# Norm intermediates and the squared ReLU move from SBUF to PSUM, and scale and shift become three instructions

## The chip, the core and the metric

The kernel runs on one core of one Trainium2 chip. The metric is the device time of one execution in microseconds (us); the time of a kernel is the median of its runs. The engines are named as the profile names them: PE (TensorE, matmuls), PEld (its weight loads), DVE (VectorE), ACT (ScalarE), POOL (GpSimd) and SP (SyncE, which issues the DMAs). A matmul writes PSUM; DVE and ACT read and write both PSUM and SBUF; POOL works here on SBUF tiles alone.

## The reference, cut to what matters

128 context tokens and 512 latent tokens, each a vector of 1024 channels, go through two layers in fp32. Layer 0 mixes tokens with a gated linear recurrence in eight heads, layer 1 with a convolution module; an MLP with 4096 hidden units follows each. Ahead of each sub-layer stands a norm with a scale and a shift that differ between context and latent tokens, and a residual with a gate closes it:

```python
def rmsnorm(x, w):
    y = xf * lax.rsqrt(jnp.mean(xf * xf, axis=-1, keepdims=True) + EPS)
    return (y * w.astype(F32)).astype(x.dtype)

hp = rmsnorm(xp, norm_mlp[i]) * (1.0 + m_ctx[4]) + m_ctx[3]     # context
hs = rmsnorm(xs, norm_mlp[i]) * (1.0 + m_lat[4]) + m_lat[3]     # latent
xs = xs + m_lat[5] * sqrelu_mlp(hs, mlp_w1[i], mlp_w2[i])

def sqrelu_mlp(h, w1, w2):
    return jnp.square(jax.nn.relu(h @ w1)) @ w2

# inside the convolution module, over the channels of each token
mu = jnp.mean(uf, axis=-1, keepdims=True)
var = jnp.mean(jnp.square(uf - mu), axis=-1, keepdims=True)
uf = (uf - mu) * lax.rsqrt(var + EPS) * ln_g.astype(F32) + ln_b.astype(F32)
return jax.nn.silu(uf).astype(h.dtype) @ w_pw2
```

## The kernel before

Activations lie channel by token: 8 tiles of 128 channels (index k), 640 token columns, context first. The columns are worked in two halves, A and B: 320 and 320 up to the first norm of layer 1, and 304 and 336 behind it. Half A holds all 128 context columns, so an instruction with a scale or a shift per token kind comes there in two pieces (128 and 192, or 128 and 176 columns); in half B it is one piece (`segs`).

A linear layer runs in units of 128 output channels (`half_unit`, `unit_k`): for each of 8 k, three matmuls, since weights and activations are split in a high and a low part (wh·hi + wl·hi + wh·lo; lines 180, 183, 184). A unit is 24 matmuls into one PSUM tile `ps_mm`, of which pool `mmp` has three in turn: the fourth unit's first matmul has to wait until the first unit's tile has been read for the last time. Two more PSUM pools exist: `scp` (three tiles, tag "sc", used by the recurrence and for the taps of the convolution, `ps_cv`) and `axp` (two tiles). Weights come by DMA into `rw`; ACT rounds them to `wh` (line 161), and POOL, in some stages DVE, subtracts (`wl`, line 165).

Work beside the matmuls that no unit asks for at once stands in a list `bg` of small steps (norms, the taps of the convolution, the modulation vectors of line 128), from which `between` issues some behind each unit. A planner in the framework then orders each engine's queue ahead of time by what it takes each instruction to cost; the queues run in that order.

A norm (`rms_stat`, `inv_rms`, `norm_steps`) squares each of 8 tiles on ACT into `nsq` in SBUF (line 256), adds them up on DVE in `nacc` (257), sums over channels with a matmul by ones into `ps_n` (230), takes the root on ACT into the SBUF tile `rs` (232) and the reciprocal on DVE there (233). With `by_token` the root and reciprocal are taken on a few columns, and the result is spread by matmuls into PSUM (238 to 242). Then, per k (`apply`): DVE multiplies x by `rs` into `nt` in SBUF (278), `modulate` scales and shifts in place, on DVE for half of the k (270) and on ACT for the others (268), and `split` has ACT round to the high part (169) and DVE subtract for the low part (170; tiles ah, al for half A, bh, bl for half B).

The hidden layer's evacuation (`hid_evac`): ACT takes the ReLU of `ps_mm` into the SBUF tile `hr` (703), DVE multiplies `ps_mm` by it into `hr` (704), and `split` works on `hr` (ch, cl for half A, dh, dl for half B). The residual (287) is one DVE instruction per token kind. The layer norm of the convolution (`ln_steps`) takes the channel mean with a matmul into `ps_mu` (817), copies it scaled to SBUF `mu` on ACT (819), subtracts it in eight DVE instructions (822), takes the statistics as above, and per k multiplies by `rs` (828), applies SiLU on ACT (829) and splits, all in SBUF.

Of the kernel before, what the change touches and what calls it, by code (L numbers as in the profile page):

```python
# [45 lines left out]
CUT = 304  # L46
CA = 5
TM0 = True
ND = (1, 3, 5, 7)
ND0 = (0, 2, 4, 6)  # L50
CB = 6
COLS = (((0, HALF), (HALF, NT)), ((0, CUT), (CUT, NT)))

# [16 lines left out]
def hybrid_step(ctx: ExitStack, tc: tile.TileContext, xt, vec, pos, masks, ident_in, state, c_rows, w_mod0, w_modt,  # L70
# [16 lines left out]
    mask = const.tile([P, NMASK, SB], U8, name="mask")  # L87
    ones = const.tile([P, P], F32, name="ones")
    pool.memset(ones[:], 1.0)
    eps = const.tile([P, 2], F32, name="eps")  # L90
    pool.memset(eps[:, 0:1], EPS)
    pool.memset(eps[:, 1:2], EPS * P)
# [75 lines left out]
    def split(src, hi, lo, eng=dve):  # L168
        act.copy(hi, src)  # L169
        eng.tensor_tensor(lo, src, hi.bitcast(F32), ALU.subtract)  # L170
# [55 lines left out]
    def inv_rms(tp, acc, n, by_token):  # L226

        ps = axp.tile([P, 512], F32, tag="ax", name="ps_n")
        if not by_token:
            pe.matmul(ps[:, :n], ones[:], acc, start=True, stop=True)  # L230
            rs = tp.tile([P, HW], F32, tag="rs", name="rs")
            act.activation(rs[:, :n], ps[:, :n], AF.Sqrt, bias=eps[:, 0:1], scale=1.0 / D)
            dve.reciprocal(rs[:, :n], rs[:, :n])
            return rs[:, :n]
        c = n // 4
        rc = tp.tile([P, 4], F32, tag="rc", name="rc", bufs=2)
        for i in range(4):
            pe.matmul(ps[:c, 508 + i:509 + i], acc[:, i * c:(i + 1) * c], ones[:, 0:1], start=True, stop=True)
        act.activation(rc[:c], ps[:c, 508:512], AF.Sqrt, bias=eps[:c, 0:1], scale=1.0 / D)
        dve.reciprocal(rc[:c], rc[:c])  # L240
        for i in range(4):
            pe.matmul(ps[:, i * c:(i + 1) * c], rc[:c, i:i + 1].broadcast_to([c, P]), ident[:c, :c],
                      start=True, stop=True)
        return ps[:, :n]

    def rms_stat(tp, xs, n, by_token=False):

        box = {}

        def sq(k):  # L250
            if k == 0:
                box["acc"] = tp.tile([P, HW], F32, tag="nacc", name="nacc", bufs=2)
                act.activation(box["acc"][:, :n], xs(0), AF.Square)
            else:
                t = tp.tile([P, HW], F32, tag="nsq", name="nsq", bufs=2)
                act.activation(t[:, :n], xs(k), AF.Square)
                dve.tensor_tensor(box["acc"][:, :n], box["acc"][:, :n], t[:, :n], ALU.add)  # L257

        def fin():
            box["rs"] = inv_rms(tp, box["acc"][:, :n], n, by_token)  # L260

        return box, [(0.45, lambda k=k: sq(k)) for k in range(KT)] + [(0.3 if by_token else 2.1, fin)]

    def modulate(t, layer, which, k, lo, hi, eng=act):
        for s, a, b in segs(lo, hi):
            r, sc, bi = t[:, a - lo:b - lo], amod[:, layer, which, k, s:s + 1], mvec(layer, 3 * which, k, s)
            if eng is act:
                act.activation(r, r, AF.Identity, bias=bi, scale=sc)  # L268
            else:
                eng.tensor_scalar(r, r, sc, bi, ALU.mult, ALU.add)  # L270

    def norm_steps(tp, x, layer, which, acts, lo, hi, by_token, on_dve):
        n = hi - lo
        box, steps = rms_stat(tp, lambda k: x[:, k, lo:hi], n, by_token)

        def apply(k):
            t = tp.tile([P, HW], F32, tag="nt", name="nt", bufs=2)
            dve.tensor_tensor(t[:, :n], x[:, k, lo:hi], box["rs"], ALU.mult)  # L278
            modulate(t, layer, which, k, lo, hi, dve if k in on_dve else act)
            split(t[:, :n], acts[k][0][:, :n], acts[k][1][:, :n])  # L280

        return steps + [(0.85, lambda k=k: apply(k)) for k in range(KT)]

    def residual(x, layer, chunk):
        def evac(u, half, lo, hi, ps):
            for s, a, b in segs(lo, hi):
                dve.scalar_tensor_tensor(x[:, u, a:b], ps[:, a - lo:b - lo], mvec(layer, chunk, u, s),  # L287
                                         x[:, u, a:b], ALU.mult, ALU.add)
        return evac
# [17 lines left out]
    with tc.tile_pool(name="start", bufs=1) as st:  # L307
# [78 lines left out]
        def first_norm(k0, k1):  # L386
            for k in range(k0, k1):
                pin(dve.tensor_tensor(x0[:, k], x0[:, k], rs[:], ALU.mult), int(k > 4))
                modulate(x0[:, k], 0, 0, k, 0, NT, dve)
                for half, (lo, hi) in enumerate(COLS[0]):  # L390
                    split(x0[:, k, lo:hi], h[half][k][0][:, :HALF], h[half][k][1][:, :HALF], (dve, pool)[half])

# [306 lines left out]
    def hid_evac(hid):  # L699
        def evac(u, half, lo, hi, ps):  # L700
            n = hi - lo
            r = rp.tile([P, HW], F32, tag="hr", name="hr")
            act.activation(r[:, :n], ps, AF.Relu)
            dve.tensor_tensor(r[:, :n], ps, r[:, :n], ALU.mult)  # L704
            split(r[:, :n], hid[half][u][0][:, :n], hid[half][u][1][:, :n])
        return evac

    hid = {}
# [7 lines left out]
    def mlp_out(layer, cols, group=8, done=None):  # L716
        linear(8, hid, residual(xr, layer, 5), cols, group, done=done)

    def start_norm(layer, which, half, cols, first=True, by_token=False, on_dve=ND):

        h[half] = new_act("ab"[half])
        steps = norm_steps(tp, xr, layer, which, h[half], *cols, by_token, on_dve)
        bg[:] = steps + bg if first else bg + steps
        return steps[-1]

# [4 lines left out]

    budget[1] = 3.0
    for cols in (A0, B0):
        linear(8, on, residual(xr, 0, 2), cols, done=lambda half: start_norm(0, 1, half, COLS[0][half], False, TM0, ND0))
    drain()
    with tc.tile_pool(name="wm1", bufs=1) as wmp:
        scratch = wmp.tile([P, D], F32, name="scratch")
# [73 lines left out]
    def ln_steps(half):  # L810
        n = COLS[1][half][1] - COLS[1][half][0]
        h[half] = new_act("ab"[half])
        acts = h[half]

        def mean():
            ps = axp.tile([P, 512], F32, tag="ax", name="ps_mu")
            pe.matmul(ps[:, :n], ones[:], lnb["sum"][:, :n], start=True, stop=True)
            lnb["mu"] = cv.tile([P, HW], F32, tag="mu", name="mu")
            act.activation(lnb["mu"][:, :n], ps[:, :n], AF.Copy, scale=1.0 / D)

        def sub(k):
            dve.tensor_tensor(lnb["y"][:, k, :n], lnb["y"][:, k, :n], lnb["mu"][:, :n], ALU.subtract)  # L822

        box, steps = rms_stat(tp, lambda k: lnb["y"][:, k, :n], n)

        def fin(k):
            y = lnb["y"][:, k, :n]
            dve.tensor_tensor(y, y, box["rs"], ALU.mult)
            act.activation(y, y, AF.Silu, bias=v("ln_b")[:, k:k + 1], scale=v("ln_g")[:, k:k + 1])
            split(y, acts[k][0][:, :n], acts[k][1][:, :n])  # L830

        return ([(0.5, mean)] + [(0.4, lambda k=k: sub(k)) for k in range(KT)] + steps
                + [(0.8, lambda k=k: fin(k)) for k in range(KT)])
# [135 lines left out]
```

## Time and profile before

| | before |
|---|---|
| time, median of 3 runs (lowest to highest) | 1619.97 us (1619.37 to 1620.06) |
| the profiled execution | 1616.84 us |
| its span, first to last instruction | 1614.9 us |
| mean granted clock of TensorE | 0.989 |
| PE busy | 1578.3 us (98%) |
| DVE busy | 1249.4 us (77%) |
| ACT busy | 761.9 us (47%) |
| POOL busy | 694.0 us (43%) |
| DMA | 240.11 MB, mean 149 GB/s |

PE is busy nearly all the time, so the parts of the span that are not its own are read from what PE waited for, stretch by stretch, and from what the engine that it waited for had in its queue there. Times of day in the text ("at 811 us") count from the start of the span.

### The profile page before, as it was taken

How to read it: one execution, taken by the hardware profiler on the slowest of the kernel's cores; microseconds unless marked ns; L12 is line 12 of the kernel's file. 1: busy time of each engine (PE TensorE's matmuls, PEld its weight loads, DVE VectorE, ACT ScalarE, POOL GpSimd, SP SyncE). 2: the span in 40 equal slices, each digit the busy share in tenths (PEclk: the TensorE clock that was granted, in tenths of full speed). 3: DMA queues.
4: the chain of work that ended last, by engine and by line, in shares of the span. 5: the costliest groups of instructions: out<-in, count | busy, mean ns of one | idle time of the engine just before them, and what ended most of it. 6: DMA issues, size and time to landing. Idle time of an engine off the chain costs nothing.

```text
span 1614.9 us, 32111 instructions
## 1 busy us (share of the span) xinstructions
PE 1578.3 (98%) x12810; PEld 1536.0 (95%) x12810; DVE 1249.4 (77%) x2222; ACT 761.9 (47%) x1227; POOL 694.0 (43%) x863
## 2 busy tenths in 40 slices
PE   8999999999999999999999999999999899999997
PEld 6899999988899999999999999989999899999997
DVE  5788888878738998788789997899999686555544
ACT  3566666665446313344454334764344554334321
POOL 3100000000484765555978888789898710000000
PEclk7999999999999999999999999999999999999998
DMA  9333333333253556766544444345454344444401
GB/s 360 129 112 113 112 112 113 112 109 103 101 190 122 181 183 224 235 225 208 169 144 144 156 146 145 129 134 169 157 164 148 122 153 158 144 144 144 144 27 66
DMA packets 71302, 240.11 MB, mean 149 GB/s; under 512 B 7792, under 2 KB 14576, under 8 KB 70128
## 3 DMA queue, kind: packets, MB, share of 16 engines
q1 hardware_dynamic: 71152, 238.06, 44.4%
q8 instruction: 101, 1.65, 0.4%
q14 instruction: 49, 0.40, 0.1%
HBM read 234.36 MB, written 3.67 MB: 147 GB/s over the span
## 4 chain that ended last, share of the span: by engine, by line
PE 76%; DVE 17%; POOL 2%; ACT 2%; issue 2%; DMA 0%; SPq 0%; DVEq 0%; POOLq 0%; ACTq 0%
PE ps_mm L180 23%; PE ps_mm L184 22%; PE ps_mm L183 22%; DVE ps_cv L794 3%; POOL wl L165 2%; DVE scratch L128 2%; PE ps_sc L504 2%; DVE nt L278 1%; DVE nacc L257 1%; DVE cl L170 1%; PE ps_u L588 1%; DVE hr L704 1%; DVE nt L270 1%; DVE yc L822 1%; DVE al L170 1%
## 5 line engine op out<-in xcount | busy, mean ns | idle before, releaser
L165 POOL TENSOR_TENSOR wl<-rw,wh 128x256 fp32r<-128x256 f32 x808 | 668.8, 861 | 568.1 <-ACT wh L161 561.6
L161 ACT CAST wh<-rw 128x1024 fp32r<-128x1024 f32 x334 | 348.4, 1046 | 314.4 <-PE ps_mm L184 230.8
L180 PE MATMUL ps_mm<-bh,wh 128*128 128x320 f32 (+1 forms) x1000 | 317.8, 318 | 2.8 <-ACT nt L268 2.6
L180 PE MATMUL ps_mm<-ah,wh 128*128 128x320 f32 (+1 forms) x1000 | 311.6, 312 | 1.9 <-ACT ah L169 1.1
L183 PE MATMUL ps_mm<-bh,wl 128*128 128x320 f32 (+1 forms) x1000 | 311.4, 312 | 0.0
L184 PE MATMUL ps_mm<-bl,wh 128*128 128x320 f32 (+1 forms) x1000 | 310.8, 311 | 0.0
L184 PE MATMUL ps_mm<-al,wh 128*128 128x320 f32 (+1 forms) x1000 | 308.0, 308 | 1.7 <-DVE al L170 1.7
L183 PE MATMUL ps_mm<-ah,wl 128*128 128x320 f32 (+1 forms) x1000 | 308.0, 308 | 0.0
L794 DVE SCALAR_TENSOR_TENSOR ps_cv<-ub,vt,ps_cv 128x319 f32<-128x319 f32 (+1 forms) x464 | 228.7, 555 | 0.4
L165 DVE TENSOR_TENSOR wl<-rw,wh 128x1024 fp32r<-128x1024 f32 x132 | 168.7, 1280 | 39.6 <-ACT wh L161 39.6
L180 PEld LDWEIGHTS ps_mm<-ah,wh 128*128 128x128 f32 x1000 | 188.6, 189 | 7.3 <-issue 3.4
L180 PEld LDWEIGHTS ps_mm<-bh,wh 128*128 128x128 f32 x1000 | 188.0, 188 | 5.7 <-ACT nt L268 2.8
L183 PEld LDWEIGHTS ps_mm<-ah,wl 128*128 128x128 f32 x1000 | 188.5, 188 | 3.2 <-issue 2.6
L184 PEld LDWEIGHTS ps_mm<-al,wh 128*128 128x128 f32 x1000 | 188.6, 189 | 3.1 <-DVE al L170 2.2
L183 PEld LDWEIGHTS ps_mm<-bh,wl 128*128 128x128 f32 x1000 | 187.9, 188 | 0.5
L184 PEld LDWEIGHTS ps_mm<-bl,wh 128*128 128x128 f32 x1000 | 188.1, 188 | 0.1
L287 DVE SCALAR_TENSOR_TENSOR xr<-ps_mm,mod,xr 128x128 f32<-128x128 f32 (+2 forms) x240 | 97.8, 434 | 112.3 <-PE ps_mm L184 111.9
L180 PE MATMUL ps_mm<-ch,wh 128*128 128x320 f32 (+1 forms) x576 | 176.8, 307 | 4.4 <-ACT ch L169 2.3
L180 PE MATMUL ps_mm<-dh,wh 128*128 128x320 f32 (+1 forms) x576 | 180.7, 314 | 0.0
L184 PE MATMUL ps_mm<-dl,wh 128*128 128x320 f32 (+1 forms) x576 | 180.0, 313 | 0.0
L183 PE MATMUL ps_mm<-dh,wl 128*128 128x320 f32 (+1 forms) x576 | 179.7, 312 | 0.0
L184 PE MATMUL ps_mm<-cl,wh 128*128 128x320 f32 (+1 forms) x576 | 176.7, 307 | 1.8 <-DVE cl L170 1.8
(209 smaller groups left out, 2550.4 us busy)
## 6 DMA issues: line engine op xcount, KB each, us to landing
rw<-in_w_mlp SPq DMA_DIRECT2D x230, 512.0 KB, 3.4
wm<-in_w_modt SPq DMA_DIRECT2D x80, 512.0 KB, 4.2
rw<-in_w_pw SPq DMA_DIRECT2D x48, 512.0 KB, 3.3
rw<-in_w_in SPq DMA_DIRECT2D x40, 512.0 KB, 3.5
wmb<-in_w_mod SPq DMA_DIRECT2D x8, 1024.0 KB, 10.1
rw<-in_w_out SPq DMA_DIRECT2D x16, 512.0 KB, 3.4
x<-in_xt SPq DMA_DIRECT2D x8, 320.0 KB, 5.7
xr<-in_xt SPq DMA_DIRECT2D x8, 320.0 KB, 6.2
```

Source lines behind the costliest of these rows:

```text
L128: tc.keep_in_program_order(dve.scalar_tensor_tensor(scratch, box["w"][:], 1.0, cbs[:, s], ALU.mult, ALU.mult, accum_out=raw_m[:, i, s:s + 1]))
L161: act.copy(wh[:], rw[:])
L165: eng.tensor_tensor(wl[:, k:k + step], rw[:, k:k + step], wh[:, k:k + step].bitcast(F32), ALU.subtract)
L170: eng.tensor_tensor(lo, src, hi.bitcast(F32), ALU.subtract)
L180: first = pe.matmul(ps[:, :n], wh[:, k, :], hi[:, :n], start=k == 0, stop=False)
L183: pe.matmul(ps[:, :n], wl[:, k, :], hi[:, :n], start=False, stop=False)
L184: pe.matmul(ps[:, :n], wh[:, k, :], lo[:, :n], start=False, stop=k == KT - 1)
L257: dve.tensor_tensor(box["acc"][:, :n], box["acc"][:, :n], t[:, :n], ALU.add)
L270: eng.tensor_scalar(r, r, sc, bi, ALU.mult, ALU.add)
L287: dve.scalar_tensor_tensor(x[:, u, a:b], ps[:, a - lo:b - lo], mvec(layer, chunk, u, s), x[:, u, a:b], ALU.mult, ALU.add)
L504: pe.matmul(ps[r:r + w, t * w:(t + 1) * w], x[:, s0:s0 + w], y[:, t0:t0 + w], start=True, stop=True, tile_position=(0, r))
L794: dve.scalar_tensor_tensor(box[i][:, :m], u[:, j:j + m], w, box[i][:, :m], ALU.mult, ALU.add)
```

## The change

Five things change, and no DMA and no matmul of a linear layer with them.

- The squares `nsq` go to a PSUM tile of pool `scp`, and the add reads them from there. 
- In the norm that is not by token, root and reciprocal are taken in place in `ps_n`, and `apply` and the others read the result from PSUM. 
- `apply` is three instructions per piece: DVE multiplies x by the scale and by `rs` into a PSUM tile `nt` of `scp`; ACT adds the shift and rounds to the high part; DVE adds the shift again and subtracts the high part. `modulate` on ACT, and the choice of engine by k, are gone. 
- In `hid_evac` DVE's product goes back into `ps_mm`, and ACT's rounding and DVE's subtraction read it there. 
- In the layer norm the mean comes from a matmul by 1/1024 (`ones_d`) and is read from `ps_mu` itself; the normed value and its SiLU lie in a tile of `scp`.

```diff
@@ const
+    ones_d = const.tile([P, P], F32, name="ones_d")
+    pool.memset(ones_d[:], 1.0 / D)
@@ inv_rms
-            rs = tp.tile([P, HW], F32, tag="rs", name="rs")
-            act.activation(rs[:, :n], ps[:, :n], AF.Sqrt, bias=eps[:, 0:1], scale=1.0 / D)
-            dve.reciprocal(rs[:, :n], rs[:, :n])
-            return rs[:, :n]
+            act.activation(ps[:, :n], ps[:, :n], AF.Sqrt, bias=eps[:, 0:1], scale=1.0 / D)
+            dve.reciprocal(ps[:, :n], ps[:, :n])
+            return ps[:, :n]
@@ rms_stat
-                t = tp.tile([P, HW], F32, tag="nsq", name="nsq", bufs=2)
+                t = scp.tile([P, 512], F32, tag="sc", name="nsq")
                 act.activation(t[:, :n], xs(k), AF.Square)
-                dve.tensor_tensor(box["acc"][:, :n], box["acc"][:, :n], t[:, :n], ALU.add)
+                dve.tensor_tensor(box["acc"][:, :n], t[:, :n], box["acc"][:, :n], ALU.add)
@@ modulate (now on DVE alone, used by the first norm alone)
-            if eng is act:
-                act.activation(r, r, AF.Identity, bias=bi, scale=sc)
-            else:
-                eng.tensor_scalar(r, r, sc, bi, ALU.mult, ALU.add)
+            dve.tensor_scalar(r, r, sc, bi, ALU.mult, ALU.add)
@@ norm_steps
         def apply(k):
-            t = tp.tile([P, HW], F32, tag="nt", name="nt", bufs=2)
-            dve.tensor_tensor(t[:, :n], x[:, k, lo:hi], box["rs"], ALU.mult)
-            modulate(t, layer, which, k, lo, hi, dve if k in on_dve else act)
-            split(t[:, :n], acts[k][0][:, :n], acts[k][1][:, :n])
+            t = scp.tile([P, 512], F32, tag="sc", name="nt")
+            for s, a, b in segs(lo, hi):
+                c = slice(a - lo, b - lo)
+                sh = mvec(layer, 3 * which, k, s)
+                dve.scalar_tensor_tensor(t[:, c], x[:, k, a:b], amod[:, layer, which, k, s:s + 1], box["rs"][:, c],
+                                         ALU.mult, ALU.mult)
+                act.activation(acts[k][0][:, c], t[:, c], AF.Identity, bias=sh)
+                dve.scalar_tensor_tensor(acts[k][1][:, c], t[:, c], sh, acts[k][0][:, c].bitcast(F32),
+                                         ALU.add, ALU.subtract)
@@ hid_evac
             act.activation(r[:, :n], ps, AF.Relu)
-            dve.tensor_tensor(r[:, :n], ps, r[:, :n], ALU.mult)
-            split(r[:, :n], hid[half][u][0][:, :n], hid[half][u][1][:, :n])
+            dve.tensor_tensor(ps, ps, r[:, :n], ALU.mult)
+            split(ps, hid[half][u][0][:, :n], hid[half][u][1][:, :n])
@@ ln_steps
-            pe.matmul(ps[:, :n], ones[:], lnb["sum"][:, :n], start=True, stop=True)
-            lnb["mu"] = cv.tile([P, HW], F32, tag="mu", name="mu")
-            act.activation(lnb["mu"][:, :n], ps[:, :n], AF.Copy, scale=1.0 / D)
+            pe.matmul(ps[:, :n], ones_d[:], lnb["sum"][:, :n], start=True, stop=True)
+            lnb["mu"] = ps
...
-            y = lnb["y"][:, k, :n]
-            dve.tensor_tensor(y, y, box["rs"], ALU.mult)
+            t = scp.tile([P, 512], F32, tag="sc", name="lt")
+            y = t[:, :n]
+            dve.tensor_tensor(y, lnb["y"][:, k, :n], box["rs"], ALU.mult)
             act.activation(y, y, AF.Silu, bias=v("ln_b")[:, k:k + 1], scale=v("ln_g")[:, k:k + 1])
             split(y, acts[k][0][:, :n], acts[k][1][:, :n])
```

## Rows read from the trace of the kernel before

**Rows 1.** The page's first part: busy time, share of the span, instructions of PE.

```profile
PE 1578.3 (98%) x12810; PEld 1536.0 (95%) x12810; DVE 1249.4 (77%) x2222; ACT 761.9 (47%) x1227; POOL 694.0 (43%) x863
```

**Rows 2.** PE's waits in 500:520, 540:580, 800:830, 1000:1070, 1240:1265: us in total, times, longest.

```profile
PE ps_n L238 <- DVE nacc L257: 2.6, 1, 2.6
...
PE ps_mm L180 <- DVE hr L704: 0.8, 1, 0.8
...
PE ps_mm L184 <- DVE al L170: 1.7, 2, 1.2
PE ps_mm L180 <- ACT ah L169: 1.1, 1, 1.1
...
PE ps_mm L180 <- ACT nt L268: 2.6, 1, 2.6
PE ps_n L230 <- DVE nacc L257: 1.7, 1, 1.7
...
PE ps_mm L180 <- ACT ch L169: 2.3, 1, 2.3
PE ps_n L230 <- DVE nacc L257: 1.1, 1, 1.1
```

**Rows 3.** Busy time by stretch: us; PE, PEld, DVE, ACT, POOL; then PEclk, DMA, GB/s.

```profile
506.60:510.00 3.40, 3.40 (x16) 3.40 (x15) 0.49 (x1) 0.90 (x2) 3.16 (x5) 0.50 0.90 325
813.80:817.20 3.40, 2.84 (x11) 2.84 (x12) 3.36 (x8) 2.57 (x5) 2.40 (x3) 0.50 0.49 154
```

**Rows 4.** Single lines: duration in ns, min/median/max, first and last start, forms.

```profile
L822 DVE TENSOR_TENSOR yc<-yc,mu x16: 460/1006/1048, 1000.2 to 1252.9; 128x304 f32<-128x304 f32 x8, 128x336 f32<-128x336 f32 x8
L278 DVE TENSOR_TENSOR nt<-xr,ps_n x16: 473/480/489, 482.3 to 520.3; 128x320 f32<-128x320 f32 x16
```

**Rows 5.** Timeline of DVE, then of POOL, around 1291: start us, us, instruction.

```profile
1291.00 7.97 DVE L257 TENSOR_TENSOR nacc<-nacc,nsq 128x336 f32<-128x336 f32 x1 [1.03 <-ACT nsq L256]
...
1289.51 9.09 POOL L165 TENSOR_TENSOR wl<-rw,wh 128x256 fp32r<-128x256 f32 x13
```

**Rows 6.** Groups by line and shape, whole span: busy us, mean ns, idle before.

```profile
L794 DVE SCALAR_TENSOR_TENSOR ps_cv<-ub,vt,ps_cv 128x319 f32<-128x319 f32 x232 | 111.9, 547 | 0.2
...
L287 DVE SCALAR_TENSOR_TENSOR xr<-ps_mm,mod,xr 128x128 f32<-128x128 f32 x80 | 27.8, 347 | 53.0 <-PE ps_mm L184 52.9
...
L287 DVE SCALAR_TENSOR_TENSOR xr<-ps_mm,mod,xr 128x192 f32<-128x192 f32 x40 | 16.3, 407 | 0.0
```

**Rows 7.** DVE's groups in 801.9:822.0, same columns.

```profile
L278 DVE TENSOR_TENSOR nt<-xr,rs 128x320 f32<-128x320 f32 x8 | 4.7, 591 | 0.0
L170 DVE TENSOR_TENSOR al<-nt,ah 128x320 fp32r<-128x320 f32 x8 | 4.6, 618 | 0.5 <-ACT ah L169 0.5
L170 DVE TENSOR_TENSOR dl<-hr,dh 128x320 fp32r<-128x320 f32 x4 | 3.8, 946 | 0.8 <-ACT dh L169 0.8
L270 DVE TENSOR_SCALAR nt<-nt,amod,mod 128x192 f32<-128x192 f32 x4 | 2.8, 691 | 0.0
L270 DVE TENSOR_SCALAR nt<-nt,amod,mod 128x128 f32<-128x128 f32 x4 | 2.3, 564 | 0.1
```

**Rows 8.** DVE's groups in 1037.4:1062.5, same columns.

```profile
L170 DVE TENSOR_TENSOR bl<-nt,bh 128x320 fp32r<-128x320 f32 x8 | 6.6, 834 | 0.1
L278 DVE TENSOR_TENSOR nt<-xr,rs 128x320 f32<-128x320 f32 x8 | 5.6, 736 | 0.0
L257 DVE TENSOR_TENSOR nacc<-nacc,nsq 128x304 f32<-128x304 f32 x6 | 5.6, 933 | 0.5 <-ACT nsq L256 0.5
L270 DVE TENSOR_SCALAR nt<-nt,amod,mod 128x320 f32<-128x320 f32 x4 | 2.7, 678 | 0.0
```

**Rows 9.** Busy time in the stretch 513:546, columns as in Rows 3.

```profile
513.00:546.00 33.00, 33.00 (x227) 33.00 (x226) 32.34 (x59) 14.80 (x30) 20.39 (x16) 1.00 0.37 128
```

**Rows 10.** Timeline of DVE, then of PE, around 520: a low part, a unit's first matmul.

```profile
521.04 0.48 DVE L170 TENSOR_TENSOR cl<-hr,ch 128x320 fp32r<-128x320 f32 x1
...
520.26 0.31 PE L180 MATMUL ps_mm<-bh,wh 128*128 128x320 f32 x1
```

More of the change, by code (lines that the diff above doesn't have):

```diff
@@ L48 @@
 TM0 = True
-ND = (1, 3, 5, 7)
-ND0 = (0, 2, 4, 6)
 CB = 6
@@ L262, in rms_stat, with modulate, norm_steps @@
         return box, [(0.45, lambda k=k: sq(k)) for k in range(KT)] + [(0.3 if by_token else 2.1, fin)]
-    def modulate(t, layer, which, k, lo, hi, eng=act):
+    def modulate(t, layer, which, k, lo, hi):
         for s, a, b in segs(lo, hi):
             r, sc, bi = t[:, a - lo:b - lo], amod[:, layer, which, k, s:s + 1], mvec(layer, 3 * which, k, s)
-            if eng is act:
-                act.activation(r, r, AF.Identity, bias=bi, scale=sc)
-            else:
-                eng.tensor_scalar(r, r, sc, bi, ALU.mult, ALU.add)
-    def norm_steps(tp, x, layer, which, acts, lo, hi, by_token, on_dve):
+            dve.tensor_scalar(r, r, sc, bi, ALU.mult, ALU.add)
+    def norm_steps(tp, x, layer, which, acts, lo, hi, by_token):
         n = hi - lo
@@ L388, in first_norm @@
                 pin(dve.tensor_tensor(x0[:, k], x0[:, k], rs[:], ALU.mult), int(k > 4))
-                modulate(x0[:, k], 0, 0, k, 0, NT, dve)
+                modulate(x0[:, k], 0, 0, k, 0, NT)
                 for half, (lo, hi) in enumerate(COLS[0]):
@@ L717, in mlp_out, with start_norm @@
         linear(8, hid, residual(xr, layer, 5), cols, group, done=done)
-    def start_norm(layer, which, half, cols, first=True, by_token=False, on_dve=ND):
+    def start_norm(layer, which, half, cols, first=True, by_token=False):
         h[half] = new_act("ab"[half])
-        steps = norm_steps(tp, xr, layer, which, h[half], *cols, by_token, on_dve)
+        steps = norm_steps(tp, xr, layer, which, h[half], *cols, by_token)
         bg[:] = steps + bg if first else bg + steps
@@ L732, in hybrid_step @@
     for cols in (A0, B0):
-        linear(8, on, residual(xr, 0, 2), cols, done=lambda half: start_norm(0, 1, half, COLS[0][half], False, TM0, ND0))
+        linear(8, on, residual(xr, 0, 2), cols, done=lambda half: start_norm(0, 1, half, COLS[0][half], False, TM0))
     drain()
```

## The prediction

> **What bounds the kernel now.** I read the page's first part, then PE's waits by stretch, then DVE's queue in each stretch. PE is busy for 98% of the span [rows 1], so no change to DVE or ACT is worth its own busy time: it can give back only what PE stood still for, behind DVE or ACT. The waits that the change touches lie in six stretches [rows 2]. S1 (500 to 520 us, norm of half B ahead of the first MLP): 2.6 us for the last add of the squares. S2 (540 to 580, first MLP): 0.8 for a PSUM tile that DVE had not released. S3 (800 to 830, norm of half A): 1.7 and 1.1 for low and high parts. S4 (1000 to 1012, layer norm): 1.7 for the adds. S5 (1037 to 1062, norm of half B): 2.6. S6 (1245 to 1260, second layer norm): 2.3 for a rounding that stood behind DVE's queue, 1.1 for the adds. [...]
>
> In all but S2 the late one is DVE, or ACT behind DVE, and the second thing to see is why DVE is late. One and the same subtraction with both inputs in SBUF takes 460 ns or 1006 to 1048 ns [rows 4]; the extreme is an add that began at 1291.00, beside a POOL train of 9.09 us that had begun at 1289.51, and lasted 7.97 us, until that train was nearly through [rows 5]. So DVE and POOL stand in each other's way when DVE reads two SBUF tiles. With one input in PSUM a product of 320 columns takes 473 to 489 ns, sixteen times out of sixteen [rows 4], and the 232 taps of 319 columns, issued while POOL subtracts weights, average 547 ns [rows 6]. The change takes the second SBUF input from nearly every DVE instruction of the norms and of the MLP's evacuation.
>
> **The change part by part.** Prices: a scalar_tensor_tensor with SBUF and PSUM inputs and a PSUM output, which is what `apply` now issues, takes 547 ns at 319 columns, and with a PSUM input 347 at 128 and 407 at 192 [rows 6]; a tensor_tensor with a PSUM input 0.48 [rows 4].
>
> S3. The eight `apply` of half A cost DVE 4.7 + 4.6 + 2.8 + 2.3 = 14.4 us, the four low parts of hidden units between them 3.8 [rows 7]. After: 8 × 2 × (0.347 + 0.407) = 12.1 and 4 × 0.48 = 1.9. DVE is through 2.3 + 1.9 = 4.2 us sooner, against waits of 1.7 + 1.1 = 2.8. In two pieces per k the three instructions form a chain through one PSUM tile, DVE, ACT, DVE and again, and if the second piece has to wait for ACT's reading of the first, some 0.4 us per k could come back (3.2 in all, on the worst order). Bounds 0 and 2.8; I take 2.0, near the upper end, since three `nt` tiles are in turn instead of two and DVE can work on the next k meanwhile.
>
> S1. The same eight `apply`, but here `rs` is in PSUM already at 0.48 [rows 4] instead of 0.591, so 2.3 - 8 × 0.11 = 1.4 sooner, and about 0.5 for each of half B's adds that meets POOL (1.0 against 0.48 [rows 4]), two or three of them. Wait 2.6, bounds 0.5 and 2.6; I take 2.0.
>
> The half clock. 16 matmuls instead of 23 are 1.0 us late in S1, up to 1.5 at 0.267 against 0.145 us each; S3 the same. For S5, where PE stood as long, they show none, so it may go or stay: bounds 0 and 3.0, I take 1.5.
>
> S4. Eight subtractions at 0.48 instead of about 1.0 where POOL runs [rows 4], and the copy `mu` on ACT gone: over 3 us sooner, wait 1.7. I take 1.5, bounds 0.5 and 1.7.
>
> S5. 6.6 + 5.6 + 5.6 + 2.7 = 20.5 us [rows 8] become 16 × 0.547 + 6 × 0.48 = 11.6: 8.9 sooner, wait 2.6, all of it. Bounds 1.0 and 2.6.
>
> S6. As S4: with about five of its eight subtractions in the slow mode (the median of all sixteen is 1006 ns [rows 4]) 2.6, plus the copy, plus a low part of a hidden unit in the slow mode, 0.5; about 3.5 sooner against 2.3 + 1.1 = 3.4. I take 3.2, bounds 1.0 and 3.4.
>
> The hidden units. DVE's product stays at 0.48; the low part reads one PSUM tile and is spared the collision, which is worth something only where DVE is late. But `ps_mm` is now released behind the low part, not behind the product: a rounding and a subtraction later, 1.0 us at least. Queued behind that tile is PE's fourth unit. A unit takes 24 × 0.145 = 3.5 us [rows 9], so the tile has two units, 7.0 us, from the end of its matmuls. Through most of the kernel that holds. From 513 to 546 it doesn't: DVE is busy for 32.34 of 33.00 us [rows 9], and the worst low part ends at 521.04 + 0.48 = 521.52, while the unit that needs the tile began at 520.26 [rows 10]: 1.26 us short. PE, once late, is late for the following units too, so the shortfalls don't add up. In S2 the wait for such a release (0.8) gets longer by up to 1.0. Bounds 0 and 2.3 lost; I take 0.8, since the planner sees the later release too.
>
> What no row shows: a reciprocal in PSUM in place (seven of them), squares that ACT writes to PSUM, ACT reading a bias from SBUF and its data from PSUM. By the nearest rows, 0.48 in PSUM against 0.46 alone in SBUF [rows 4], each is within 0.05 us either way; 0, and within ±0.5 over the stretches. The extra memset on POOL at the start stands behind the one that PE waits for: 0. SP's queue and its transfers are not moved; POOL's subtractions get shorter, which nobody waits for. The norms where POOL is idle (about 1320 and 1590) gain nothing: one piece costs 2 × 0.547 instead of two or three shorter ones.
>
> [...]
>
> **The sum.** 2.0 + 1.5 + 1.5 + 2.6 + 3.2 + 2.0 - 0.8 = 12.0 us. The profiled execution took 1616.84 us (span 1614.9, 1.9 around it), 3.1 below the median of the runs, 1619.97. After: 1604.8 profiled, 1608.0 as a median.
>
> **The rivals.**
> 1. All of it, and the half clock gone: 2.6 + 2.8 + 3.0 + 1.7 + 2.6 + 3.4 = 16.1, no loss at the tiles, and small waits of the same kind: about 1602. For it: in each stretch DVE saves about what PE waits or more.
> 2. Half of it. PE's order is fixed ahead: in S1 the matmul for the statistics stands in the middle of a unit and holds up what is ready behind it. Planned anew with other costs, such matmuls may again be put where DVE is just late. 1619.97 - 6 = 1614.
> 3. No change (0 to 3 us): the waits are set by where the planner puts things and move with it, or the collision passes to other pairs (the weights' and line 128's instructions still read two SBUF tiles): 1618.5. Against it: S5's 8.9 us.
> 4. Slower, by the tiles' release. If in the first MLP's 16 units the low part is ordered behind the steps of line 128, each unit is late by the 1.26 us of the worst one [rows 10]: 16 × 1.26 = 20.2, less 12.0 + 0.8 gained elsewhere: 1627. It decides from about 1.0 us per unit on, that is, once the low parts end more than 8 us behind their unit's matmuls as a rule. For it: DVE is 98% busy there. Against it: DVE's work there shrinks, and PE, being late, gives it time.
>
> **How the numbers follow.** Forecast 0.46 (1604 to 1612), rival 1 0.13, rival 2 0.18, rival 3 0.14, rival 4 0.09. Likeliest is the forecast: 1608.0. The range runs from 1600.0, a little below rival 1, to 1619.0, and leaves out rival 4 and a part of rival 3. A measurement of this kernel tells 0.2% (3.2 us) from no change. Faster by more: forecast, rivals 1 and 2, 0.77; same: rival 3, 0.14; slower: rival 4, 0.09.
>
> **What would show it.** Right: DVE's adds, products and low parts last about 0.5 us beside POOL too, with no second mode at 1.0; PE's waits for `nacc`, for `ah`, `al` and `bh`, and for `ch` in S6 are under 1 us; PEclk is 1.00 in both stretches of [rows 3]. Wrong: scalar_tensor_tensor rows at 0.8 us or more beside POOL (then the collision is not one of two SBUF inputs); DVE idle in S3 with ACT as releaser (the chain through one tile); PE waits for `ps_mm` with a low part as releaser between 513 and 580 (rival 4).

## The result and the profile after

| | before | changed |
|---|---|---|
| time, median (lowest to highest) | 1619.67 us (1618.63 to 1620.06) | 1594.54 us (1593.53 to 1596.30) |
| ratio, with its 95% interval | | 0.985 (0.984 to 0.986) |
| the profiled execution, its span | 1616.84, 1614.9 us | 1593.53, 1591.8 us |

The kernel became faster, as forecast, but by 25.1 us and not by 12.0; the time lies 5.5 us below the lower end of the range.

The page of the changed kernel, first part and the clock's row in 40 slices (answers [rows 1]):

```profile
PE 1569.5 (99%) x12810; PEld 1531.5 (96%) x12810; DVE 1186.1 (75%) x2234; ACT 744.9 (47%) x1213; POOL 655.8 (41%) x864
...
PEclk8999999999999999999999999999999999999998
```

DVE lost 63 us of busy time (from 1249.4), POOL 38 with the same subtractions: each had been in the other's way. PE gives back only what it stood still for. All that it still waits for between 490 and 1270 us, where [rows 2] named eight waits (line, releaser: us in total, times, longest):

```profile
PE ps_mm L180 <- DVE cl L170: 2.2, 1, 2.2
PE ps_mm L180 <- ACT ah L279: 0.8, 1, 0.8
```

The second is a remainder. The first is new, and it is rival 4's. The two stretches that answer to [rows 3], found 10 us earlier (columns as there), run at a granted clock of 1.00, where they had 0.50 (in before, two matmuls in a row into `ps_mm` start 0.267 us apart there and 0.147 at 1.00, from 513 to 546 us, by the median):

```profile
504.80:508.20 3.40, 3.40 (x29) 3.40 (x28) 3.26 (x7) 2.41 (x4) 0.00 (x0) 1.00 0.45 154
803.80:807.20 3.40, 3.38 (x24) 3.12 (x23) 2.89 (x10) 2.19 (x6) 2.24 (x4) 1.00 0.45 146
```

Single lines (ns, min/median/max), for [rows 4] and the add of [rows 5]; the last is the low part of the hidden units:

```profile
L822 DVE TENSOR_TENSOR yc<-yc,ps_mu x16: 464/484/505, 989.5 to 1237.6; 128x304 f32<-128x304 f32 x8, 128x336 f32<-128x336 f32 x8
...
L256 DVE TENSOR_TENSOR nacc<-nsq,nacc x70: 465/491/508, 449.6 to 1580.9; 128x320 f32<-128x320 f32 x28, 128x304 f32<-128x304 f32 x21, 128x336 f32<-128x336 f32 x21
...
L170 DVE TENSOR_TENSOR cl<-ps_mm,ch x64: 459/477/495, 505.6 to 1517.0; 128x320 fp32r<-128x320 f32 x32, 128x304 fp32r<-128x304 f32 x32
```

The second mode at 1.0 us is gone from all three, and the add that had once lasted 7.97 us [rows 5] has a maximum of 508 ns. DVE's groups in S3 (793 to 812) and S5 (1020 to 1050), the answers to [rows 7, 8]:

```profile
L277 DVE SCALAR_TENSOR_TENSOR nt<-xr,amod,ps_n 128x192 f32<-128x192 f32 x7 | 3.0, 422 | 0.2
L280 DVE SCALAR_TENSOR_TENSOR al<-nt,mod,ah 128x192 fp32r<-128x192 f32 x6 | 2.5, 413 | 0.7 <-ACT ah L279 0.7
L277 DVE SCALAR_TENSOR_TENSOR nt<-xr,amod,ps_n 128x128 f32<-128x128 f32 x7 | 2.5, 351 | 0.0
L280 DVE SCALAR_TENSOR_TENSOR al<-nt,mod,ah 128x128 fp32r<-128x128 f32 x7 | 2.4, 342 | 0.0
...
L280 DVE SCALAR_TENSOR_TENSOR bl<-nt,mod,bh 128x320 fp32r<-128x320 f32 x8 | 4.3, 547 | 0.7 <-ACT bh L279 0.6
L277 DVE SCALAR_TENSOR_TENSOR nt<-xr,amod,ps_n 128x320 f32<-128x320 f32 x8 | 4.1, 549 | 0.0
```

The means of 342 to 422 and of 547 to 549 ns are the prices that [rows 6] had (347, 407, 547), with POOL busy for 14.0 of the 19 us of S3 and 24.7 of the 30 of S5.

**Where the time went.** Every kernel here has 9456 matmuls into `ps_mm`, so a stretch of PE can be fixed by their numbers: the time between the starts of two of them, counted in the trace. (This counts what PE lost in full; a wait row shows only what lay between the modelled end of one matmul and the next.) In us, with the two half changes that are told of below:

| matmuls | what is there | before | hidden units only | norms only | changed |
|---|---|---|---|---|---|
| to 177 | the start | 97.1 | 97.0 | 94.9 | 95.1 |
| 2090 to 2350 | S1, begin of the first MLP | 44.0 | 45.4 | 42.8 | 43.8 |
| 2350 to 2712 | S2 | 55.9 | 53.1 | 55.5 | 53.1 |
| 2712 to 4065 | rest of that MLP | 200.1 | 199.4 | 200.0 | 199.3 |
| 4065 to 4333 | S3 | 44.9 | 46.0 | 41.1 | 40.7 |
| 5390 to 5574 | S4 | 30.0 | 30.0 | 28.0 | 28.0 |
| 5644 to 5902 | S5 | 42.0 | 44.8 | 37.5 | 37.5 |
| 5902 to 7059 | MLP of layer 1 | 163.0 | 162.5 | 162.6 | 162.5 |
| 7059 to 7260 | S6 | 35.1 | 33.5 | 32.0 | 29.0 |
| 177 to 9456 | all behind the start | 1505.6 | 1506.3 | 1490.8 | 1484.4 |

Behind the start 21.2 us are gone, 21.1 of them in these stretches. Each column is one execution. That of before lay 2.8 us below its kernel's median and that of the hidden units only (1617.71) 4.1 above, so what the hidden units bring by themselves is read from the medians below, not from these two columns.

### The profile page after: what moved, and what is told of

The parts are those of the page before. It is cut to its first block, busy times and chain, and to the rows that moved or that the text cites. A ratio compares the mean times of both kernels' runs of the same rounds, so it can differ in the third digit from the quotient of the medians.

```text
span 1591.8 us, 32155 instructions
## 1 busy us (share of the span) xinstructions
PE 1569.5 (99%) x12810; PEld 1531.5 (96%) x12810; DVE 1186.1 (75%) x2234; ACT 744.9 (47%) x1213; POOL 655.8 (41%) x864
## 3 DMA queue, kind: packets, MB, share of 16 engines
q1 hardware_dynamic: 71152, 238.06, 44.8%
## 4 chain that ended last, share of the span: by engine, by line
PE 86%; DVE 6%; POOL 2%; ACT 2%; DMA 2%; issue 2%; SPq 0%; DVEq 0%; POOLq 0%; ACTq 0%
PE ps_mm L180 27%; PE ps_mm L184 26%; PE ps_mm L183 26%; POOL wl L165 2%; PE ps_sc L505 2%; DMA rw<-in_w_in 1%; PE ps_u L589 1%; DVE scr L128 1%; ACT xy L515 1%; DVE a L521 0%; PE ssq L461 0%; DVE a L523 0%; PE ps_o L604 0%; DVE nt L277 0%; DMA x<-in_xt 0%
## 5 line engine op out<-in xcount | busy, mean ns | idle before, releaser
L165 POOL TENSOR_TENSOR wl<-rw,wh 128x256 fp32r<-128x256 f32 x808 | 630.7, 815 | 584.9 <-ACT wh L161 584.5
L161 ACT CAST wh<-rw 128x1024 fp32r<-128x1024 f32 x334 | 350.0, 1050 | 326.6 <-PE ps_mm L184 257.6
L165 DVE TENSOR_TENSOR wl<-rw,wh 128x1024 fp32r<-128x1024 f32 x132 | 166.7, 1265 | 43.8 <-ACT wh L161 43.8
```

What stands on the lines that cost most here:

```text
L161: act.copy(wh[:], rw[:])
L165: eng.tensor_tensor(wl[:, k:k + step], rw[:, k:k + step], wh[:, k:k + step].bitcast(F32), ALU.subtract)
```

## The experiments

**Is it the collision with POOL?** The theory says that the change is worth what DVE lost beside POOL. Its rival says that shorter or fewer instructions are worth something by themselves. So I took the collision away instead of the second SBUF input: in both kernels POOL's subtractions are left out from the 41st weight tile on, and the high part takes the place of the low part `wl` (that part of the computation is missing; the number of matmuls is the same).

```diff
+            if eng is pool and i >= 40:
+                split_w.append((wh, wh))
+                continue
             wl = wpool.tile([P, KT, P], F32R, tag="wl", name="wl")
```

> The kernel before, with POOL's subtractions for the weights' low parts left out from the 41st weight on: the matmul of the low part reads the high part instead, so the output is not the reference's; matmuls, DMAs, DVE and ACT are as before. If DVE was late because two SBUF inputs collide with POOL, the subtractions of the mean and the products of the norms all last under 0.55 us, PE's waits in the six stretches are mostly gone, and the time is 1596 to 1604 us. If the change wins by fewer and shorter instructions, or by the planner's new order, this kernel keeps its waits and stays at 1612 us or more.

> The kernel after, with the same subtractions of POOL left out in the same way. If the collision is the cause, it gains nothing or little beside the kernel after (1591 to 1595 us) and lies within 6 us of the kernel before without POOL. If the instructions' number or the order is the cause, it lies 15 us or more below the kernel before without POOL.

Measured: before without POOL 1586.09 us (ratio to before 0.980, 0.978 to 0.981), the changed kernel without POOL 1591.17 (0.983, 0.981 to 0.984). What PE waits for between 490 and 1270 us in the kernel before, once POOL is silent, and two of its lines:

```profile
PE ps_n L233 <- DVE nacc L260: 0.4, 1, 0.4
...
L825 DVE TENSOR_TENSOR yc<-yc,mu x16: 468/487/509, 980.5 to 1222.7; 128x304 f32<-128x304 f32 x8, 128x336 f32<-128x336 f32 x8
...
L173 DVE TENSOR_TENSOR cl<-hr,ch x64: 462/480/493, 500.8 to 1508.6; 128x320 fp32r<-128x320 f32 x32, 128x304 fp32r<-128x304 f32 x32
```

The same instructions on the same two SBUF tiles take 487 and 480 ns, and of the eight waits of [rows 2] one is left, at 0.4 us, with no other edit. PE, DVE and ACT run the same instructions in the same order as in before, one by one, so no new plan of the queues is behind this; and PE in before never waits for a `wl` of POOL, so late weights are not behind it either. The collision was the cause of the waits. DVE is busy for 1156.3 us there, 93 less than in before; the change took 63 of these. Without it the change gains nothing: its time is 5.1 us longer. In the two profiled executions, 6.5 us apart, 3.8 lie between matmuls 2090 and 2350 (43.7 against 39.9 us), where a wait of 2.2 us for `cl` stands, as the one seen above, and 2.5 in the start (95.2 against 92.7 us to matmul 177), which is chance, as a later run shows.

**Which half brings how much?** One kernel takes the squared ReLU of the change alone, the other all but it:

```diff
-            dve.tensor_tensor(r[:, :n], ps, r[:, :n], ALU.mult)
-            split(r[:, :n], hid[half][u][0][:, :n], hid[half][u][1][:, :n])
+            dve.tensor_tensor(ps, ps, r[:, :n], ALU.mult)
+            split(ps, hid[half][u][0][:, :n], hid[half][u][1][:, :n])
```

> The kernel before with one part of the change, the squared ReLU left in its matmul tile. By the prediction the later release of that tile costs about 0.8 us and the spared collision of the low parts is worth little: 1618 to 1621 us. If the hidden units' low parts were a large part of DVE's lateness, 1610 us or less. If the release decides, 1623 us or more, with PE waiting for ps_mm behind a low part.

> The kernel after with the squared ReLU as before (product, rounding and subtraction in the SBUF tile hr) and all of the norms as after. By the prediction 1594 to 1600 us, without the wait of PE for a hidden tile's release in the first MLP (2.2 us after). If both parts are needed to bring DVE in time, 1603 us or more.

Measured: hidden units only 1613.62 us (0.997, 0.996 to 0.998), norms only 1599.59 (0.989, 0.987 to 0.990). The halves add up: 5.9 (by the interval 2.6 to 7.0) and 19.9, against 25.1. From norms only to the whole change it is 5.1 by the medians, 6.4 by the table, above all in S2 and S6. The row behind it, low parts of the hidden units in the kernel before:

```profile
L170 DVE TENSOR_TENSOR cl<-hr,ch x64: 461/500/1071, 511.6 to 1540.4; 128x320 fp32r<-128x320 f32 x32, 128x304 fp32r<-128x304 f32 x32
```

and what PE waits for with the norms only, in S2 (534 to 590) and S6 (1225 to 1245); with the hidden units changed too, no wait is left in either:

```profile
PE ps_mm L180 <- DVE xr L288: 1.3, 1, 1.3
PE ps_mm L180 <- DVE hr L705: 0.5, 1, 0.5
...
PE ps_mm L180 <- DVE hr L705: 1.9, 3, 1.2
```

The residual `xr` and the product `hr` read one SBUF tile and one PSUM tile, and do not collide themselves (in before the residual of 128 columns takes at most 354 ns, beside POOL or not, the product at most 494 beside it and 508 without); they stand in DVE's queue behind low parts that do.

**PSUM or fusion?** In the changed kernel, once with `rs` and `nt` back in SBUF and the three fused instructions kept, once with the separate steps of before and `nt` in PSUM:

```diff
@@ fused, in SBUF (rs likewise)
...
+            t = tp.tile([P, HW], F32, tag="nt", name="nt", bufs=2)
@@ separate, in PSUM
...
             t = scp.tile([P, 512], F32, tag="sc", name="nt")
+            dve.tensor_tensor(t[:, :n], x[:, k, lo:hi], box["rs"], ALU.mult)
...
+                if k % 2:
+                    dve.tensor_scalar(r, r, sc, bi, ALU.mult, ALU.add)
+                else:
+                    act.activation(r, r, AF.Identity, bias=bi, scale=sc)
+            split(t[:, :n], acts[k][0][:, :n], acts[k][1][:, :n])
```

> The changed kernel with the norm's factor rs and the tile nt of apply back in SBUF: the three fused instructions stay, their inputs don't lie in PSUM. Theory collision (the gain is the second SBUF input taken away): S1, S3 and S5 lose most of what they gained (about 3 + 4.6 + 4.5 us of excess in PE's steady pace), S4 and S6, the hidden units and the squares in PSUM keep theirs: 1604 (1600 to 1608), and the first product of apply lasts 0.8 us or more beside POOL. Theory fusion (the gain is fewer instructions on DVE): 1595 +- 2, as the changed kernel.

> The changed kernel with apply in separate steps as before (product, scale and shift on DVE for odd k and on ACT for even, rounding, subtraction), but with nt in PSUM. Theory collision: no instruction of apply has two SBUF inputs, so it keeps nearly all of the gain although DVE has more instructions than with the fusion: 1596 (1593 to 1600). Theory fusion: S1, S3 and S5 fall back by up to 12 us in all: 1604 to 1607.

Measured: fused in SBUF 1598.70 us (0.987, 0.985 to 0.989), separate in PSUM 1595.79 (0.985, 0.983 to 0.986). The second has the changed kernel's time, so the fusion brings nothing that can be measured here. The first fell between the two expectations, and the stretches tell why. S3 is back at 44.9 us, all of its gain lost, and PE waits there (790 to 830) for

```profile
PE ps_mm L184 <- DVE al L281: 2.2, 4, 1.2
PE ps_mm L180 <- ACT ah L280: 1.1, 2, 0.7
```

but S5 stays at 38.0 although its instructions collide. DVE's groups there (1024 to 1050):

```profile
L281 DVE SCALAR_TENSOR_TENSOR bl<-nt,mod,bh 128x320 fp32r<-128x320 f32 x8 | 6.6, 850 | 0.0
L278 DVE SCALAR_TENSOR_TENSOR nt<-xr,amod,rs 128x320 f32<-128x320 f32 x8 | 6.5, 845 | 0.0
L257 DVE TENSOR_TENSOR nacc<-nsq,nacc 128x304 f32<-128x304 f32 x7 | 3.3, 465 | 1.0 <-ACT nsq L256 1.0
```

850 and 845 ns instead of 547 and 549: the fused form collides as well, and costs 13.1 us against 14.9 for the three groups of [rows 8] that it stands for. The adds, which read the squares from PSUM, take 465 ns instead of 933 [rows 8]. That the two together were enough for S5 is likely, but no run separates them. S1 keeps its time too (43.3): its norm is by token and reads the factor from PSUM in all these kernels.

A second SBUF input is not the only thing that collides. `modulate` on DVE has one tile as its input, in SBUF, and writes it back in place. Its row in before, in before with POOL silent, and with `nt` in PSUM:

```profile
L270 DVE TENSOR_SCALAR nt<-nt,amod,mod x36: 333/446/864, 483.1 to 1337.8; 128x128 f32<-128x128 f32 x12, 128x192 f32<-128x192 f32 x8, 128x320 f32<-128x320 f32 x8, 128x176 f32<-128x176 f32 x4
...
L273 DVE TENSOR_SCALAR nt<-nt,amod,mod x36: 340/375/452, 476.4 to 1306.0; 128x128 f32<-128x128 f32 x12, 128x192 f32<-128x192 f32 x8, 128x320 f32<-128x320 f32 x8, 128x176 f32<-128x176 f32 x4
...
L278 DVE TENSOR_SCALAR nt<-nt,amod,mod x36: 408/476/627, 482.7 to 1311.1; 128x128 f32<-128x128 f32 x12, 128x192 f32<-128x192 f32 x8, 128x320 f32<-128x320 f32 x8, 128x176 f32<-128x176 f32 x4
```

At 192 columns, counted one by one in the traces, it takes 791 to 806 ns in before where a subtraction of POOL runs beside it, and 368 to 377 where none does. In PSUM it takes 474 to 478, beside POOL or not: it is spared the collision there, at a price of some 100 ns.

**The layer norm alone.** The changed kernel with that part undone:

```diff
...
-            lnb["mu"] = ps
+            lnb["mu"] = cv.tile([P, HW], F32, tag="mu", name="mu")
+            act.activation(lnb["mu"][:, :n], ps[:, :n], AF.Copy, scale=1.0 / D)
...
-            t = scp.tile([P, 512], F32, tag="sc", name="lt")
-            y = t[:, :n]
-            dve.tensor_tensor(y, lnb["y"][:, k, :n], box["rs"], ALU.mult)
+            y = lnb["y"][:, k, :n]
+            dve.tensor_tensor(y, y, box["rs"], ALU.mult)
```

> The changed kernel with the layer-norm part alone undone (mean copied to the SBUF tile mu, normed value and SiLU in SBUF). It sizes S4 and S6, for which the forecast took 1.5 + 3.2 = 4.7 us. By the excess over PE's steady pace, before against after, they were worth 2.0 + 6.0 = 8.0: then 1602.5 +- 1.5, with the waits for nacc at about 1000 and for ch and nacc at about 1250 back. If the single waits of the rows of before are right and the rest came from the neighbours: 1599 +- 1.

Measured: 1598.67 us (0.989, 0.987 to 0.991), against 1592.40 for the changed kernel on the same chip. By the stretches it is worth 3.0: S4 lasts 28.4 us instead of 28.0, S6 31.6 instead of 29.0. Another 2.9 between the two profiled executions (1598.47 and 1591.70) lie in the start (96.8 against 93.9 us to matmul 177), which is chance, as the next runs show; whether the medians lie 6.3 apart for the same reason is not shown. So of S4's 2.0 us only 0.4 come from the layer norm. The other 1.6 are most likely the squares in PSUM, since the wait in S4 was for their adds [rows 2], but no run takes them alone. What PE waits for in S6 (1240 to 1252):

```profile
PE ps_mm L180 <- DVE xr L288: 1.3, 1, 1.3
PE ps_n L230 <- DVE nacc L256: 0.9, 1, 0.9
```

**The start, and before once more.** The changed kernel had been 2.0 us ahead by matmul 177, before any norm. One kernel is before with the new constant tile alone, the other the changed kernel again:

```diff
+    ones_d = const.tile([P, P], F32, name="ones_d")
+    pool.memset(ones_d[:], 1.0 / D)
```

> The kernel before with the second constant tile alone (its memset on POOL at the start, read by nobody). The changed kernel's matmuls run 2.0 us ahead of before's by 48 us, before any norm has run, and one half-clock stretch of 6.8 us at the start is gone. Theory A: the gain comes from the order that the planner found at the start, which any change of POOL's queue there may shift: then this kernel's start moves too, 1617.5 +- 1. Theory B: the start is better only because the norms' steps behind it are planned otherwise: then this kernel is like before, 1619.5 +- 1, with both half-clock stretches at the start.

> The changed kernel once more, as it is: the measure for the next kernel on the same chip, 1594.5 +- 1. It also tells whether the start differs from one execution to the next: PE's order there is the same in all kernels so far, so if the start's 2 us are chance, its 600th matmul begins anywhere between 82 and 87 us, and not always at 84.5.

Measured: with the memset 1621.21 us (1.000, 0.998 to 1.002), no change; the changed kernel again 1592.40 (0.985, 0.983 to 0.988). PE's order up to 442 us of before is the same in all kernels here, and matmul 177 starts anywhere from 92.7 to 97.7 us: 93.9 in the changed kernel's second execution, 97.7 in a kernel that is the changed one there. The rows for 24 to 36 us of before, the changed kernel, the same again, and that other one:

```profile
24.00:36.00 12.00, 9.70 (x54) 8.39 (x53) 10.69 (x17) 2.29 (x6) 7.76 (x8) 0.64 0.90 360
...
24.00:36.00 12.00, 9.35 (x67) 7.87 (x69) 9.96 (x16) 3.08 (x6) 8.54 (x9) 0.80 0.85 337
...
24.00:36.00 12.00, 9.39 (x68) 6.92 (x68) 10.59 (x17) 2.30 (x6) 7.48 (x8) 0.85 0.93 371
...
24.00:36.00 12.00, 9.96 (x55) 8.64 (x54) 10.55 (x17) 2.46 (x5) 8.10 (x9) 0.64 0.84 335
```

Between two executions of one order PE's mean granted clock in these 12 us is 0.64 or 0.80 to 0.85, while DMA is busy for 84 to 93%. The 2 us are chance.

The memset kernel has PE's order of before, matmul for matmul, and so shows what before does in another execution: S5 lasts 44.7 us, not 42.0, S1's stretch 45.3, S6 36.4, all behind the start 1511.9 instead of 1505.6. One group of it for 1037 to 1062, the answer to the product of [rows 8]:

```profile
L280 DVE TENSOR_TENSOR nt<-xr,rs 128x320 f32<-128x320 f32 x8 | 9.6, 1234 | 0.0
```

1234 ns, where the profiled execution of before had 736. Seven of the eight last 0.48 to 1.02 us, and one, the first, 5.32. DVE's timeline around it, with the second product, and POOL's:

```profile
1041.52 5.72 DVE L280 TENSOR_TENSOR nt<-xr,rs 128x320 f32<-128x320 f32 x2
...
1035.35 11.14 POOL L167 TENSOR_TENSOR wl<-rw,wh 128x256 fp32r<-128x256 f32 x16
```

Here DVE's product lasts until POOL's train is over, and POOL's subtractions last 0.73 to 0.75 us, as if alone (0.72 to 0.74 in before with no DVE instruction beside them). In the execution of before a train of 18 stands in nearly the same place (from 1035.41), and the two engines take turns there, at up to 1.0 us for each instruction on either side. So the collision took two forms here, and which one differed from one execution to the next; what decides it stays open. The changed kernel's two executions agree within 0.4 us behind the start (1484.4 and 1484.8).

**Can the new wait be had back?** Three variants of the changed kernel (`in_sbuf` counts the units that keep their product in SBUF): all hidden units of the first MLP's first pass keep DVE's product in the SBUF tile `hr`, so that `ps_mm` is released by it; the first four alone do; and these four with half the share of line 128's steps issued behind each unit there (they run later).

```diff
-            dve.tensor_tensor(ps, ps, r[:, :n], ALU.mult)
-            split(ps, hid[half][u][0][:, :n], hid[half][u][1][:, :n])
+            q = r[:, :n] if in_sbuf[0] > 0 else ps
+            in_sbuf[0] -= 1
+            dve.tensor_tensor(q, ps, r[:, :n], ALU.mult)
+            split(q, hid[half][u][0][:, :n], hid[half][u][1][:, :n])
@@ the third
-        budget[1] = 1.8
+        budget[1] = 0.9
```

> The changed kernel, but the hidden units of layer 0's MLP that run over both halves keep DVE's product in the SBUF tile hr as before, so that ps_mm comes free behind the product and not behind the low part. If the wait of 2.2 us at 516 is the price of the late release, it is gone: 1592.3 +- 1. If DVE's queue is late there for another reason (half B's apply stands ahead of the product as well), a wait of 1.5 to 2.5 us for ps_mm stays, now with the product as releaser: 1594.5 +- 1; and if the low parts collide with POOL again, S2's old waits return: 1596 to 1597.

> The changed kernel, but the first four hidden units of layer 0's MLP alone keep DVE's product in the SBUF tile hr, so that their ps_mm is released by the product, which stands ahead of half B's apply in DVE's queue, and not by the low part behind it. If the wait of 2.2 us at 516 is the late release, and the waits of the kernel with all such units in SBUF (1.9 for hr, 1.3 for xr at 574) come from the later units: 1592 +- 1, without either. If DVE has simply too much to do between 510 and 530, the 2 us appear at another unit there: 1594.5 +- 1.

> As the kernel with the first four hidden units in SBUF, and besides with half the share (0.9 for 1.8) of line 128's steps issued behind each unit of the first MLP's first pass; they run later instead. In the kernel with the first four alone, the wait for the late low part was gone and two for the product (1.5 us) stood in its place, with DVE full. If DVE has too much to do there, they go too: the stretch of PE that lasted 42.8 us with the first four alone and 43.8 in the changed kernel (39.9 where POOL does not subtract) comes to 40 to 41.5, and the time to 1590.5 +- 1.5. If the waits come from half B's apply alone, the stretch stays at 42.5 to 43 and the time at 1592 to 1593; and where the steps run later they may cost a wait of their own.

Measured: all 1595.20 us (0.984, 0.982 to 0.986), the first four 1592.88 (0.985, 0.983 to 0.987, against 1592.40 for the changed kernel beside it), with fewer steps 1625.48 (1.003, 1.002 to 1.004). The first row is all units (515 to 580), the second the first four (515 to 530):

```profile
PE ps_mm L180 <- DVE hr L708: 1.9, 3, 1.1
PE ps_mm L180 <- DVE xr L288: 1.3, 1, 1.3
...
PE ps_mm L180 <- DVE hr L709: 1.5, 2, 1.1
```

The wait for `cl` is gone and others for the product stand in its place: 42.9 and 42.8 us between matmuls 2090 and 2350 instead of 43.8 (44.5 when run again), of the 39.9 that the kernel before takes without POOL. With all units, S2 is also back at 55.4 (norms only 55.5). A gain of 1 to 1.7 us of the first four in the trace is not told apart by the medians. The third variant tells whether line 128's steps are what fills DVE there: the stretch takes 42.2 us, so they are worth 0.6 and most of it is not theirs. But what was moved came back with interest. DVE, 800 to 845, first group, and PE's longest wait:

```profile
L128 DVE SCALAR_TENSOR_TENSOR scratch<-wm,cbs 128x1024 f32<-128x1024 f32 x18 | 24.5, 1361 | 7.5 <-DMA wm<-in_w_modt 7.5
...
PE ps_mm L180 <- ACT ah L279: 23.5, 5, 10.9
```

Eighteen of the steps were left over when layer 1's first norm came, and it had to wait: S3's stretch takes 73.3 us. No version measured here beats the changed kernel; what else holds PE for some 2 us between 503 and 530 stays open.

## Why the prediction was right in its mechanism and wrong in its size

The mechanism held at each point that it named. None of the rows above has a second mode, the fused forms cost what [rows 6] said, the waits of S3 to S6 are under 1 us, both half-clock stretches are gone, and in the chain of `apply` in S3 DVE is idle behind ACT for 0.7 us only. It was too narrow in one point: the scale and shift in place in SBUF, with a single SBUF input, collides as well (at 192 columns in before 791 to 806 ns beside POOL, 368 to 377 without it), and the change took that away too. For two SBUF inputs the runs show 487 ns without POOL and up to 1048 beside it for the same subtraction. With an input in PSUM the subtraction is not dearer: 484 ns, against these 487 from SBUF with POOL silent. The scale and shift in place is the one form above that is dearer in PSUM (474 to 478 ns).

Two readings of rows were not right. The add of [rows 5] ended at 1298.97, 0.37 us behind the train and not before its end. And DVE is the late one in S2 as well: the wait of 0.8 in [rows 2] is for its product. Three rows of before that the sum left out, in S2 (534 to 590), S6 (1235 to 1270) and S5 (1030 to 1072):

```profile
PE ps_mm L180 <- DVE xr L287: 1.3, 1, 1.3
...
PE ps_mm L184 <- DVE cl L170: 0.9, 1, 0.9
...
PE ps_mm L180 <- DVE xr L287: 0.8, 1, 0.8
```

The miss of 13.1 us (25.1 measured, 12.0 forecast) has four parts, rounded; the first two are terms of the sum, the other two belong to the executions that were profiled:

- **The hidden units, 7.2 us.** This is the step that failed. Forecast -0.8, measured +6.4 (1490.8 against 1484.4 behind the start; 5.1 and 5.9 by the medians). I wrote that the low part is spared the collision, "which is worth something only where DVE is late", and then priced it at nothing in S2, where the waits of 0.8 and 1.3 were for DVE's queue, and in S6, where 0.9 was for a low part itself. The table has it: S2 2.4, S6 3.0, the two other MLP stretches 0.8. The counted loss was real: rival 4's mechanism occurred, once, and S1's stretch is 1.0 longer with it.
- **The norms, 2.0 us.** The terms came to 12.8 (S1 2.0, S3 2.0, clock 1.5, S4 1.5, S5 2.6, S6 3.2); with the norms only the trace lost 14.8. S5 was worth 4.5 and S3 3.8, because I summed the wait rows that I had picked, and a stretch loses more than these: the further wait for `xr` in S5 (0.8), the short stalls that no wait row shows, and the half clock in S3. In the memset kernel's execution S5 loses 2.7 more, so its size depends on the execution of before. S4 was 2.0, but for another reason than the one I gave: only 0.4 is the mean and what follows it. S6 was 3.1, of which 2.6 are the layer norm. S1 was too high: 1.2 instead of 2.0 and half of the clock's 1.5 (an estimate from 0.267 against 0.145 us a matmul: the runs show both half-clock stretches gone, and none takes them alone), probably because the time that it won ran into the first MLP's full DVE.
- **The start, 2.0 us:** chance, as shown.
- **The median, 1.8 us.** The execution of before that the sum went by lay 2.8 below the median, the changed kernel's 1.0. I carried the 3.1 over as a constant. It is not one: one order of PE took 1505.6 and 1511.9 us behind the start in two executions, and the start differs by some us in either kernel.

The release of the tile, forecast at 1.26 us short, is this in the changed kernel (DVE's timeline from 508 us, then ACT's and PE's: start, us, instruction):

```profile
508.88 0.47 DVE L705 TENSOR_TENSOR ps_mm<-ps_mm,hr 128x320 f32<-128x320 f32 x1
510.62 1.47 DVE L277 SCALAR_TENSOR_TENSOR nt<-xr,amod,ps_n 128x320 f32<-128x320 f32 x3 [1.27 <-PE ps_n L241]
512.00 1.63 DVE L280 SCALAR_TENSOR_TENSOR bl<-nt,mod,bh 128x320 fp32r<-128x320 f32 x3
513.55 1.47 DVE L277 SCALAR_TENSOR_TENSOR nt<-xr,amod,ps_n 128x320 f32<-128x320 f32 x3
514.92 1.46 DVE L280 SCALAR_TENSOR_TENSOR bl<-nt,mod,bh 128x320 fp32r<-128x320 f32 x3
516.30 1.01 DVE L277 SCALAR_TENSOR_TENSOR nt<-xr,amod,ps_n 128x320 f32<-128x320 f32 x2
517.21 0.49 DVE L170 TENSOR_TENSOR cl<-ps_mm,ch 128x320 fp32r<-128x320 f32 x1
...
509.38 0.43 ACT L169 CAST ch<-ps_mm 128x320 fp32r<-128x320 f32 x1 [1.22 <-DVE ps_mm L705]
...
517.85 0.39 PE L180 MATMUL ps_mm<-bh,wh 128*128 128x320 f32 x1 [2.23 <-DVE cl L170]
```

The product was there at 509.35, its low part ended at 517.70: between them the queue holds all eight first steps of half B's `apply` and six of their low parts. For 1.27 us of that time DVE stood idle, waiting for PE's spread of the norm's factor, although the rounded part `ch` was ready at 509.81: it was the low part's place in the queue that made it late, not a lack of time on DVE alone. I had argued that PE, once late, is late for the next units too; this held, as it happened to one tile. What I had not seen is that the steps ahead of the low part would be the norm's and not line 128's.

The rivals. "All of it" was nearest in mechanism and still 7.5 us short, since it too had the hidden units at nothing. "Half", "no change" and "slower" fell. My range ended at 1600 because its best case added up the very wait rows that were incomplete.

## What to carry to other kernels

Where POOL runs elementwise work on SBUF beside DVE, give each DVE instruction at most one SBUF input, with the other one in PSUM, and do not leave a scale and shift in place in SBUF either. Here, beside POOL, the subtraction of the mean took up to 1048 ns from two SBUF tiles and at most 505 with one input in PSUM, the scale and shift of 192 columns 791 to 806 in SBUF and 474 to 478 in PSUM. Together this was worth 25 us in 1620 here, and fusing the instructions nothing measurable beyond it. Size such a change by what PE loses in the stretch, counted between two numbered matmuls and over more than one execution, not by picked wait rows; and price every instruction that leaves the collision, the frequent small ones of the main loop above all. A PSUM tile that serves as scratch is held longer (for `ps_mm` PE waited 2.2 us once): look up what stands in the queue ahead of its last reader.

## What the hardware showed that I had not expected

- Taking POOL's subtractions away from the kernel before gained 33.4 us (1619.48 on that chip, 1586.09), so the collision held about 2% of a kernel whose PE is 98% busy.
- One order of PE and ACT, with DVE's the same but for one instruction at 10 us, had 736 and 1234 ns as the mean of the same eight products, in two executions, because one product waited out a train of POOL. On one chip the kernel before scattered from 1614.4 to 1622.0 us over 9 executions and the changed one from 1591.7 to 1598.4 over 5, so that a narrower spread without the collision is not shown.
- A reciprocal of 304 to 336 columns costs 2.16 us in PSUM and 2.14 in SBUF (medians of seven), and the rest of what no row of before had shown (ACT's squares into PSUM, its rounding with a bias) made no wait of over 0.8 us.
